# A kernel of two transformer blocks with 32 experts: a fixed order for the loop over pairs of experts, another beginning of the experts' stage, and weights in chunks of half a matrix

## The chip, the cores and the metric

One core of a Trainium2 chip. The metric is the time of one execution on the device in microseconds; the kernel before ran three times: 1050.86, 1051.72 and 1053.38 us, median 1051.72.

## The reference

Two transformer blocks over 256 tokens of width 1024, all in f32. The first has two kinds of attention and a gated FFN with a convolution. The second has two kinds of attention and then a mixture of experts, and only that is touched:

```python
h2 = modulate(rmsnorm(x, g_ffn), shift_ffn, scale_ffn)
group = argmax(softmax(h2 @ w_group))                 # 4 groups
p, e = top_k(softmax((h2 @ w_expert)[group]), 2)      # 2 of the 8 experts of the group
y = sum over the 2 of: weight * ((silu(h2 @ w_gate[e]) * (h2 @ w_up[e])) @ w_down[e])
out = rmsnorm(x + gate_ffn * y, g_final)
```

There are 32 experts; w_gate and w_up of one are 1024 x 512, w_down is 512 x 1024, 2 MB each: 192 MB (of 1,048,576 bytes) in all, each read once.

## The kernel before, in words

All large weights come through one ring of 1 MB buffers (8 KB a partition). `plan` (L405) lists the chunks in the order of their use, `pump` (L150) issues the next chunk's load on SyncE's queue as soon as a buffer is free, and `done` gives a chunk's buffer back when its last product is issued. SyncE's queue is in program order; the order on the other engines is chosen by the tile framework's scheduler when the kernel is built, except that instructions given to `pin` keep their program order among each other. The ring has 10 buffers and gets others as earlier stages give them up: 17 ahead of the experts' stage, an 18th when the transposed x (`xT`, buffer WHL[0]) has been read, a 19th when x has been added to the accumulators.

The experts go in 16 pairs. A chunk of a pair is a quarter of one matrix of both experts: `w_pair` (L344 issues) takes for each partition one run of 4 KB of each expert, that is two rows k of gate or up, or one row of down. A pair has 12 chunks: four of gate, four of up, four of down.

`moe` (L1480 on) begins with the residual (L1497), the squares of x and their root (`squares`, `root`: L235, L240, L241), and the transposes of x on TensorE (L206) whose copies to SBUF (L1508, L1510) give xT. `route` (L1303 on) has per block of 128 tokens: logits by 16 products with xT, then a chain of VectorE steps (L1310 to L1327), a short product that counts tokens per expert, and their ranks `rk` (L1336). A generator is stepped by the string `'a2 q1 a4 ...'`. Pair 0 gets its 2 x 64 token places by products with a selection matrix (`selects` L1523, `row`), in f32, as soon as the ranks are there. For the other pairs `normed` (L1534, L1535) makes x times its root as a high and a low fp32r part, `places` (L1545) makes the 0/1 matrix `hot`, and `gather` multiplies the two and lets ScalarE modulate the result into `xt` (L1539). Pairs are gathered in groups (0), (1,2), (3,4), ..., (13,14), (15).

The loop over pairs then has for pair pr, as written: gate products (`times_x`, 32 TensorE instructions), half 0 of `combine` of pair pr-1 (products that add the weighted output into the four accumulator banks), `weighted` of that pair's half 1 (L1475 to L1477), up products, half 1 of `combine`, silu and product (`gated`, L1593, L1594), `slots` (transposes of `hot` and the slots' weights, L1573, L1576), `places` of the next group, `act_T` (four transposes and two copies, L1604), `gather` of the next group in every second pair, `down` (32 instructions). Two pairs of PSUM banks, 4 to 7, take turns. For pair 15 a branch comes first (`rest_of_experts`, for experts with more than 64 tokens; it isn't entered here), and then the load of the last gain. The final norm follows (L1703 to L1708). TensorE's instructions are all recorded at the helpers' lines, L203 for products and L206 for transposes.

Of the kernel before, what the change touches and what calls it, by code (L numbers as in the profile page):

```python
# [111 lines left out]
class Kernel:  # L112
# [12 lines left out]


# [75 lines left out]
    def mm(self, out, lhsT, rhs, start, stop):  # L202
        return self.nc.tensor.matmul(out, lhsT, rhs, start=start, stop=stop, skip_group_check=True)  # L203

    def tr(self, out, in_, ident):
        return self.nc.tensor.transpose(out, in_, ident)  # L206
# [139 lines left out]

    def w_tiles(self, src, r0):
# [57 lines left out]
    def plan(self):  # L405
# [1063 lines left out]
    def weighted(self, ps, w, gate, hf, y):  # L1469
# [5 lines left out]
        nc.vector.scalar_tensor_tensor(tmp[:n], ps, w, gate[:n, cs], op0=ALU.mult, op1=ALU.mult)  # L1475
        nc.scalar.activation(y[:, 0], tmp[:n], AF.Copy)  # L1476
        nc.vector.tensor_tensor(y[:, 1], tmp[:n], y[:, 0], op=ALU.subtract)  # L1477

    def moe(self):
# [37 lines left out]
        def selects(pr, tb, pin=lambda i: i):  # L1517

            s = self.t([128, 128], "sel", tag="diag", bufs=2)
            sel[tb] = s  # L1520
            for e in range(2):
                n = 2 * pr + e
                pin(nc.vector.scalar_tensor_tensor(s[:, e * 64:e * 64 + 64], self.iota1, self.rk[:, tb, n:n + 1],  # L1523
                                                   r2[:, tb:tb + 1].to_broadcast([128, 64]), op0=ALU.is_equal,
                                                   op1=ALU.mult))
# [53 lines left out]
        def times_x(pr, n, b):  # L1579
            ps = self.bank(b)  # L1580
            for k in range(KT):
# [5 lines left out]
                if k % 2:  # L1587
                    self.done(c)
# [180 lines left out]
```

## Time and profile before

| | |
|---|---|
| median of 3 runs | 1051.72 us |
| the profiled execution's own time | 1051.73 us |
| its span, first to last instruction | 1049.9 us |
| TensorE busy, share of the span | 983.1 us, 94% |
| VectorE, ScalarE, GpSimd busy | 515.7, 407.3, 47.1 us |
| mean granted TensorE clock | 0.983 |
| bytes moved by DMA | 313.51 MB, mean 299 GB/s |

The busy times are sums over stages with different limits. The experts' stage begins at 558 us. What limits it is read from its own stretches: how full the DMA stream is, what TensorE waits for, and what comes last. A share of DMA above 1 means that packets of one engine overlap a little. Times in the rows are us from the start of the span.

### The profile page before, as it was taken

The page shows a single profiled execution, that of the slowest core. Times are in us where ns is not written, and L with a number is a line of the kernel's source. Part 1 is how long each engine was busy: PE and PEld are TensorE (multiplying, and loading weights), DVE is VectorE, ACT ScalarE, POOL GpSimd, SP SyncE. Part 2 cuts the span into 40 slices and gives each one's busy share as a digit, 9 for nine tenths or more (in the row PEclk, how much of TensorE's full clock was granted, in tenths as well). Part 3 has the DMA queues.
Part 4 walks back from the last instruction along what each step waited for, and adds up shares of the span by engine and source line. Part 5 has one row for each costly group of instructions (what it writes and reads, how often), then busy time and mean ns, then how long its engine had stood idle before and what let it go on. Part 6 is the DMA issues. An engine that isn't in the chain of part 4 may idle for free. (4 is left out here: it accounts for less than half of the span.)

```text
span 1049.9 us, 14498 instructions
## 1 busy us (share of the span) xinstructions
PE 983.1 (94%) x5815; PEld 672.5 (64%) x5815; DVE 515.7 (49%) x940; ACT 407.3 (39%) x751; POOL 47.1 (4%) x48
## 2 busy tenths in 40 slices
PE   5999899999999998899987999999899999999996
PEld 5997599999999996789766535334343334333342
DVE  5658688979889876656796111111111110111112
ACT  5566566555555555455653311111020202011022
POOL 2000200000000001000061000000000000000000
PEclk9999999999999999899998999999999999999999
DMA  7964655967777867554644799999999999999995
GB/s 202 368 236 128 226 202 165 315 230 256 267 250 235 287 230 269 204 164 151 254 148 134 275 409 409 409 408 409 409 409 409 410 409 409 409 409 409 409 407 207
DMA packets 131519, 313.51 MB, mean 299 GB/s; under 512 B 7229, under 2 KB 59226, under 8 KB 131450
## 3 DMA queue, kind: packets, MB, share of 16 engines
q1 hardware_dynamic: 131082, 312.02, 80.0%
q0 software_dynamic: 368, 0.54, 0.3%
q8 instruction: 46, 0.75, 0.3%
q14 instruction: 23, 0.19, 0.0%
HBM read 311.89 MB, written 1.05 MB: 298 GB/s over the span
## 5 line engine op out<-in xcount | busy, mean ns | idle before, releaser
L203 PE MATMUL bank<-buf,buf 128*128 128x256 f32 (+4 forms) x4152 | 703.4, 381 | 8.0 <-DVE buf L277 2.6
L203 PEld LDWEIGHTS bank<-buf,buf 128*128 128x128 f32 (+1 forms) x4152 | 493.8, 176 | 176.4 <-issue 124.0
L178 DVE TENSOR_TENSOR buf<-buf,buf 128x1024 fp32r<-128x1024 f32 x150 | 183.2, 1222 | 57.7 <-ACT buf L176 54.7
L176 ACT ACTIVATE buf<-buf 128x1024 fp32r<-128x1024 f32 x154 | 162.2, 1054 | 93.6 <-PE bank L203 82.1
L203 PE MATMUL bank<-buf,aT 128*64 128x512 f32 x512 | 114.8, 595 | 3.3 <-ACT aT L1604 3.3
L1594 DVE TENSOR_TENSOR act<-act,bank 128x512 f32<-128x512 f32 x16 | 11.0, 688 | 208.4 <-PE bank L203 208.4
L1475 DVE SCALAR_TENSOR_TENSOR tmp<-bank,wslot,gffn 128x512 f32<-128x512 f32 x32 | 24.0, 751 | 133.0 <-PE bank L203 131.2
L203 PEld LDWEIGHTS bank<-buf,aT 128*64 128x64 f32 x512 | 37.0, 137 | 69.4 <-issue 59.6
L1593 ACT ACTIVATE act<-bank 128x512 f32<-128x512 f32 x16 | 9.6, 597 | 135.4 <-PE bank L203 135.4
L1476 ACT ACTIVATE buf<-tmp 128x512 fp32r<-128x512 f32 x32 | 20.2, 631 | 107.5 <-DVE tmp L1475 107.5
L949 ACT ACTIVATE buf<-bank,convT 128x256 f32<-128x256 f32 x64 | 36.0, 563 | 54.3 <-PE bank L203 42.5
L1539 ACT ACTIVATE buf<-bank,mod,g_ffn 128x256 f32<-128x256 f32 (+1 forms) x72 | 34.6, 538 | 48.6 <-PE bank L203 48.6
L1604 ACT ACTIVATE aT<-bank 128x256 f32<-128x256 f32 x32 | 10.5, 382 | 95.1 <-PE bank L206 95.1
L203 PE MATMUL bank<-buf,ST 128*128 128x512 f32 x128 | 38.2, 420 | 8.0 <-ACT buf L1476 7.9
L203 PEld LDWEIGHTS bank<-buf,ST 128*128 128x128 f32 x128 | 21.5, 188 | 36.8 <-ACT buf L1476 18.5
L203 PEld LDWEIGHTS bank<-hot,buf 128*128 128x128 f32 x256 | 32.0, 189 | 17.1 <-issue 8.9
L1045 DVE SCALAR_TENSOR_TENSOR bank<-buf,c,bank 128x512 f32<-128x512 f32 x56 | 41.9, 749 | 0.6 <-DMA buf<-in_w_ada_dram 0.3
L203 PE MATMUL bank<-hot,buf 128*128 128x256 f32 (+1 forms) x256 | 36.6, 290 | 3.6 <-ACT act L1593 3.6
L206 PE MATMUL bank<-base,buf 128*128 128x128 f32 x128 | 21.1, 312 | 18.0 <-DVE buf L260 7.8
L951 DVE SCALAR_TENSOR_TENSOR buf<-bank,convT,buf 128x255 f32<-128x255 f32 x64 | 30.6, 478 | 7.8 <-ACT buf L949 7.4
L206 PEld LDWEIGHTS bank<-base,buf 128*128 128x128 f32 x128 | 17.8, 176 | 21.1 <-DVE buf L260 7.8
L953 DVE SCALAR_TENSOR_TENSOR buf<-bank,convT,buf 128x254 f32<-128x254 f32 x64 | 30.6, 478 | 1.1
(203 smaller groups left out, 629.3 us busy)
## 6 DMA issues: line engine op xcount, KB each, us to landing
buf<-in_w_up_dram SPq DMA_DIRECT2D x96, 1024.0 KB, 18.1
buf<-in_w_down_dram SPq DMA_DIRECT2D x79, 1024.0 KB, 18.2
buf<-in_w_gate_dram SPq DMA_DIRECT2D x64, 1024.0 KB, 18.3
buf<-in_w_ada_dram SPq DMA_DIRECT2D x24, 1024.0 KB, 7.3
buf<-in_w_in_dram SPq DMA_DIRECT2D x18, 1024.0 KB, 9.8
buf<-in_w_out_dram SPq DMA_DIRECT2D x8, 1024.0 KB, 16.7
buf<-in_w_in_dram SPq DMA_DIRECT2D x6, 512.0 KB, 7.7
buf<-in_x_dram SPq DMA_DIRECT2D x2, 512.0 KB
```

Of the source, the lines that this page charges most:

```text
L176: pin(nc.scalar.activation(H, raw, AF.Copy))
L178: pin(engine.tensor_tensor(L, raw, H, op=ALU.subtract))
L203: return self.nc.tensor.matmul(out, lhsT, rhs, start=start, stop=stop, skip_group_check=True)
L206: return self.nc.tensor.transpose(out, in_, ident)
L949: nc.scalar.activation(c[:, s, :], u[:, s, :], AF.Identity, scale=cT[:, 128 + n:129 + n], bias=cT[:, 192 + n:193 + n])
L951: nc.vector.scalar_tensor_tensor(c[:, s, 1:], u[:, s, 0:255], cT[:, 64 + n:65 + n], c[:, s, 1:], op0=ALU.mult, op1=ALU.add)
L953: nc.vector.scalar_tensor_tensor(c[:, s, 2:], u[:, s, 0:254], cT[:, n:n + 1], c[:, s, 2:], op0=ALU.mult, op1=ALU.add)
L1045: nc.vector.scalar_tensor_tensor(p.pa, w, s, p.pa, op0=ALU.mult, op1=ALU.add)
L1475: nc.vector.scalar_tensor_tensor(tmp[:n], ps, w, gate[:n, cs], op0=ALU.mult, op1=ALU.mult)
L1476: nc.scalar.activation(y[:, 0], tmp[:n], AF.Copy)
L1539: nc.scalar.activation(xt[:, k, :n], g, AF.Identity, scale=A[:, k:k + 1], bias=B[:, k:k + 1])
L1594: nc.vector.tensor_tensor(act, act, u, op=ALU.mult)
```

## The change

Three parts. (1) The loop over pairs issues gate, silu, up, product, both halves of combine of the pair before, transposes of act, slots, gather, down and both halves of weighted, in this order, and while `self.ordered` is set every instruction of it on TensorE, VectorE and ScalarE keeps its program order. All pairs are gathered in groups of two, (0,1) to (14,15). (2) The beginning: both blocks' squares, copies and roots first; `normed` and pair 0's own f32 products are gone; instead xT is transposed back on TensorE (`back`) and its high and low parts are made from PSUM (`high`, `low`), and the first group's `gather` does all high parts first. Routing steps of the two blocks are interleaved by a new string. All four residual products come in pair 0 of the loop. (3) A chunk of gate, up and down is now half of one matrix of one expert: for each partition one run of 8 KB (`w_half`). Only the four down chunks of pair 15 keep the old form. The bytes and their order by matrix are the same.

```diff
+    def kept(self, i):
+        return self.pin(i) if self.ordered else i
...
+    def w_half(self, src, k, half):
+
+        n = src.shape[1] * k // 2
+        v = src.rearrange("(p k) c -> p (k c)", k=k)[:, half * n:half * n + n]
+
+        def load(t):
+            self.nc.sync.dma_start(t, v)
         return load
...
-                    load = self.w_pair(w[2 * pr:2 * pr + 2], k, part, 2 if (pr, n, part) == (15, "down", 3) else 1)
-                    self.experts[n, pr, part] = self.add_raw(n, load)
+                    if (pr, n) == (15, "down"):
+                        c = self.add_raw(n, self.w_pair(w[2 * pr:2 * pr + 2], k, part, 2 if part == 3 else 1))
+                        c.left = 2
+                        for e in range(2):
+                            self.experts[n, 2 * pr + e, part] = c, e * D
+                    else:
+                        e, half = part % 2, part // 2
+                        c = self.add_raw(n, self.w_half(w[2 * pr + e], k, half))
+                        c.left = k // 2
+                        for i in range(k // 2):
+                            self.experts[n, 2 * pr + e, k // 2 * half + i] = c, i * 2048 // (k // 2)
...
-        self.row_rstd(halves[0], r2[:, 0:1], self.pin)
+        pin = self.pin
         for tb in range(TB):
+            ss = self.squares(halves[tb], pin)
...
-                if tb and not half:
-                    nc.vector.tensor_copy(to, pt)
+                if half:
+                    pin(nc.vector.tensor_copy(to, pt))
                 else:
-                    self.pin(nc.scalar.activation(to, pt, AF.Copy))
-        ss = self.squares(halves[1], self.pin)
-        acc = [[self.bank(0), self.bank(1)], [self.bank(2), self.bank(3)]]
-        ST, W, sel = {}, {}, {}
-        groups = [(0,)] + [(i, i + 1) for i in range(1, 15, 2)] + [(15,)]
+                    pin(nc.scalar.activation(to, pt, AF.Copy))
+            self.root(ss, r2[:, tb:tb + 1], pin)
+        ST, W = {}, {}
+        groups = [(i, i + 1) for i in range(0, 16, 2)]
...
+        def back(tb):
+
+            pts = []
+            for half in range(2):
+                pt = self.bank((2, 3, 0, 1)[2 * tb + half], (128, 4, 128))
+                for kk in range(4):
+                    pin(self.tr(pt[:, kk, :], xT[:, half * 4 + kk, tb * 128:tb * 128 + 128], self.ident))
+                pts.append(pt)
+            return pts
+
+        def high(tb, half):
+
+            pin(nc.scalar.activation(xn[0][:, tb, half * 4:half * 4 + 4], turned[tb][half], AF.Copy,
+                                     scale=r2[:, tb:tb + 1]))
+
+        def low(tb, half):
+            ks = slice(half * 4, half * 4 + 4)
+            pin(nc.vector.scalar_tensor_tensor(xn[1][:, tb, ks], turned[tb][half], r2[:, tb:tb + 1], xn[0][:, tb, ks],
+                                               op0=ALU.mult, op1=ALU.subtract))
...
+        def gather(group, banks, first=False):
+
+            s = hot[:, where[group[0]][0]]
+            g = [self.bank(b, (128, 2, 256)) for b in banks]
+
+            def part(i, n):
+                for j in range(2):
+                    for tb in range(TB):
+                        self.mm(g[i][:, j, :], xn[n][:, tb, 2 * i + j, :], s[:, tb], n + j + tb == 0, n + tb == 2)
+            if first:
+                for i in range(4):
+                    part(i, 0)
+            for i in range(4):
+                if not first:
+                    part(i, 0)
+                part(i, 1)
+                for j in range(2):
+                    modulate(2 * i + j, g[i][:, j, :], 256)
...
         def times_x(pr, n, b):
             ps = self.bank(b)
             for k in range(KT):
-                c = self.experts[n, pr, k // 2]
                 for e in range(2):
-                    c0 = e * D + (k % 2) * 512
-                    self.mm(ps[e * 64:e * 64 + 64, :], xt[:, k, where[pr][1] + e * 64:where[pr][1] + e * 64 + 64], c.tile[:, c0:c0 + 512],
-                            k == 0, k == KT - 1)
-                if k % 2:
+                    c, c0 = self.experts[n, 2 * pr + e, k]
+                    self.mm(ps[e * 64:e * 64 + 64, :], xt[:, k, where[pr][1] + e * 64:where[pr][1] + e * 64 + 64], c.tile[:, c0:c0 + 512], k == 0, k == KT - 1)
                     self.done(c)
             return ps
...
         def down(pr, aT, banks):
             ps = [self.bank(b) for b in banks]
             for i in range(4):
-                c = self.experts["down", pr, i]
                 for hf in range(2):
                     for e in range(2):
-                        c0 = e * D + hf * 512
+                        c, c0 = self.experts["down", 2 * pr + e, i]
+                        c0 += hf * 512
                         self.mm(ps[hf][e * 64:e * 64 + 64, :], aT[i // 2][:, i % 2, e * 64:e * 64 + 64],
                                 c.tile[:, c0:c0 + 512], i == 0, i == 3)
-                self.done(c)
-            self.weighted(ps[0], W[pr], gate, 0, y[0])
-            return ps[1]
+                for e in range(2):
+                    self.done(self.experts["down", 2 * pr + e, i][0])
+            for hf in range(2):
+                self.weighted(ps[hf], W[pr], gate, hf, y[hf])
...
-        for what in 'a2 q1 a4 b1 r0 a1 b1 r1 a1 b1 s0 b1 h0 b2 b1 h1 b1 s1'.split():
+        turned = {}
+        for what in 'a4 b1 a2 t0 b1 h00 a1 t1 b1 a1 p0 h01 b3 b1 b1 p1 h10 h11 l00 l10 l01 l11'.split():
...
+            elif what[0] == "t":
+                turned[n] = back(n)
+            elif what[0] == "p":
+                self.ordered = True
+                places(groups[0], n)
+                self.ordered = False
...
+                {"h": high, "l": low}[what[0]](n, int(what[2]))
+        gather(groups[0], (6, 7, 4, 5), True)
         self.give(WHL[0])
         for tb in range(TB):
             self.expert_weights(tb, self.logits[tb])
-        normed()
-        places(groups[0])
-        second = None
+        acc = [[self.bank(0), self.bank(1)], [self.bank(2), self.bank(3)]]
+        self.ordered = True
         for pr in range(16):
-            banks, others = ((4, 5), (6, 7))[::1 if pr % 2 == 0 else -1]
-            if pr < 15:
-                g = times_x(pr, "gate", banks[0])
-            if pr:
-                combine(pr - 1, 0, False)
-                self.weighted(second, W[pr - 1], gate, 1, y[1])
-            if pr < 15:
-                u = times_x(pr, "up", banks[1])
-            if pr:
-                combine(pr - 1, 1, False)
-            else:
-                for hf in range(2):
-                    residual(1, hf)
-                self.give(X)
-                self.blocks_left()
+            banks, others = ((6, 7), (4, 5))[::1 if pr % 2 == 0 else -1]
+            group = next((gr for gr in groups if gr[0] == pr + 1), None)
             if pr == 15:
                 assert self.next_dma == len(self.chunks)
+                for hf in range(2):
+                    combine(pr - 1, hf, False)
+                self.ordered = False
                 self.rest_of_experts(xn, A, B, gate, acc, self.free[:3])
                 gfin = self.buf(self.free[3], [128, D])
                 fin = self.buf(self.free[4], [128, TB, D])
                 nc.sync.dma_start(gfin, bass.AP(tensor=a["g_final_2"].tensor, offset=a["g_final_2"].offset,
                                                 ap=[[0, 128], [1, D]]))
-                g, u = times_x(pr, "gate", banks[0]), times_x(pr, "up", banks[1])
-            act = gated(g, u)
+                self.ordered = True
+            if group:
+                for tb in range(TB):
+                    places(group, tb)
+            g = times_x(pr, "gate", banks[0])
+            act = silu(g)
+            u = times_x(pr, "up", banks[1])
+            gated(act, u)
+            if not pr:
+                for tb in range(TB):
+                    for hf in range(2):
+                        residual(tb, hf)
+                self.ordered = False
+                self.give(X)
+                self.blocks_left()
+                self.ordered = True
+            elif pr < 15:
+                for hf in range(2):
+                    combine(pr - 1, hf, False)
+            aT = act_T(pr, act, others[0])
             slots(pr, others[1])
-            group = next((gr for gr in groups if gr[0] == pr + 1), None)
-            if group:
-                places(group)
-            aT = act_T(pr, act, others[0])
             if group:
                 gather(group, banks + others)
-            second = down(pr, aT, banks)
-        self.weighted(second, W[15], gate, 1, y[1])
+            down(pr, aT, banks)
         for hf in range(2):
             combine(15, hf, True)
```

## Rows read from the trace of the kernel before

**Rows 1.** busy by stage: stretch, length, engines, clock, DMA share, GB/s

```profile
604.00:1030.00 426.00, 401.76 (x1923) 168.59 (x1920) 64.48 (x128) 65.08 (x130) 0.00 (x0) 1.00 1.03 409
```

**Rows 2.** waits of TensorE, its weight loads, 700-1000: total, times, longest

```profile
PE bank L206 <- DVE act L1594: 8.6, 10, 0.9
...
PEld bank L203 <- DMA buf<-in_w_down_dram: 1.9, 6, 0.4
```

**Rows 3.** timeline of TensorE, pairs 2 to 4: start, us, what, count

```profile
635.19 7.18 PE L203 MATMUL bank<-buf,buf 128*64 128x512 f32 x31
...
663.37 7.04 PE L203 MATMUL bank<-buf,buf 128*64 128x512 f32 x32
...
688.20 3.60 PE L203 MATMUL bank<-buf,buf 128*64 128x512 f32 x16
```

**Rows 4.** timeline of TensorE, starts of pairs 10 and 12

```profile
864.61 1.94 PE L203 MATMUL bank<-buf,buf 128*64 128x512 f32 x8
...
923.22 1.94 PE L203 MATMUL bank<-buf,buf 128*64 128x512 f32 x8
```

**Rows 5.** SyncE's issues: first after the pause, last; its landing

```profile
583.93 2.08 SPq L344 DMA_DIRECT2D buf<-in_w_up_dram  x2
...
1017.64 6.04 SPq L344 DMA_DIRECT2D buf<-in_w_down_dram  x1
...
buf<-in_w_down_dram SPq DMA_DIRECT2D x1, 512.0 KB, 19.2
```

**Rows 6.** the chain that ended last: pair 15's gate and up, its down

```profile
1015.99 13.97 PE bank L203 x64
...
1032.02 7.11 PE bank L203 x32
```

**Rows 7.** timeline of the experts' beginning, all engines

```profile
558.28 2.73 DVE L1497 SCALAR_TENSOR_TENSOR buf<-bank,rstd,buf 128x512 f32<-128x512 f32 x4 [0.82 <-POOL rstd L220]
...
561.75 2.16 ACT L1534 ACTIVATE buf<-buf,r 128x1024 fp32r<-128x1024 f32 x1
...
562.06 3.66 PE L203 MATMUL bank<-wr,buf 128*128 128x40 f32 x32
...
563.94 2.08 DVE L1535 SCALAR_TENSOR_TENSOR buf<-buf,r,buf 128x1024 fp32r<-128x1024 f32 x1 [1.44 <-ACT buf L1534]
...
565.95 0.24 DVE L1310 SCALAR_TENSOR_TENSOR logits<-bank,r,rc 128x40 f32<-128x40 f32 x1
566.22 0.49 DVE L1315 TENSOR_TENSOR rdif<-logits 128x320 f32<-128x320 f32 x1
...
576.29 0.19 DVE L1336 SCALAR_TENSOR_TENSOR rk<-bank,pick 128x32 f32<-128x32 f32 x1 [1.95 <-PE bank L203]
...
581.95 13.95 PE L203 MATMUL bank<-buf,buf 128*64 128x512 f32 x64
```

**Rows 8.** busy by stage around the routing, columns as in 1

```profile
565.00:570.00 5.00, 3.00 (x13) 1.35 (x12) 3.36 (x10) 2.86 (x3) 0.80 (x1) 1.00 0.60 193
570.00:575.00 5.00, 1.71 (x7) 1.71 (x8) 4.34 (x11) 0.00 (x0) 0.00 (x0) 0.55 0.04 16
...
580.00:585.00 5.00, 5.00 (x23) 2.88 (x24) 0.83 (x6) 4.42 (x10) 0.00 (x0) 0.93 0.05 5
```

**Rows 9.** timeline, gather of pairs 1, 2: products and modulations

```profile
599.10 3.99 PE L203 MATMUL bank<-hot,buf 128*128 128x256 f32 x32
...
600.39 3.82 ACT L1539 ACTIVATE buf<-bank,mod,g_ffn 128x256 f32<-128x256 f32 x8 [0.35 <-PE bank L203]
```

**Rows 10.** DMA packets of 8-15, 30-37, 57.5-64, 700-1000 us

```profile
DMA packets 4075, 2.05 MB, mean 293 GB/s; under 512 B 63, under 2 KB 4075, under 8 KB 4075
...
DMA packets 2417, 2.44 MB, mean 348 GB/s; under 512 B 36, under 2 KB 2417, under 8 KB 2417
...
DMA packets 1252, 2.50 MB, mean 385 GB/s; under 512 B 37, under 2 KB 37, under 8 KB 1251
...
DMA packets 31798, 122.73 MB, mean 409 GB/s; under 512 B 1869, under 2 KB 1869, under 8 KB 31786
```

More of the change, by code (lines that the diff above doesn't have):

```diff
@@ L1517, in selects @@
[L1517 to L1525, printed above, removed]
-        def row(pr, g, tb, k, start):
-            return self.mm(g[k // 4][:, k % 4, :], x[tb][:, k, :], sel[tb], start, tb == 1)
@@ L1531, in normed @@
-        def normed():
-            for tb in range(TB):
-                nc.scalar.activation(xn[0][:, tb], x[tb], AF.Copy, scale=r2[:, tb:tb + 1])
-                nc.vector.scalar_tensor_tensor(xn[1][:, tb], x[tb], r2[:, tb:tb + 1], xn[0][:, tb], op0=ALU.mult,
-                                               op1=ALU.subtract)
+                if half:
+                    pin(nc.vector.tensor_copy(to, pt))
+                else:
+                    pin(nc.scalar.activation(to, pt, AF.Copy))
+            self.root(ss, r2[:, tb:tb + 1], pin)
@@ L1547, in places @@
                                         self.rk[:, tb, 2 * group[0]:2 * group[0] + n, None].to_broadcast([128, n, 64]),
-                                        op=ALU.is_equal)
-        def gather(group, banks):
-            n = 128 * len(group)
-            each = 512 // n
-            s = hot[:, where[group[0]][0], :, :n]
-            for i in range(KT // each):
-                g = self.bank(banks[i], (128, each, n))
-                for j in range(each):
-                    for part in range(2):
-                        for tb in range(TB):
-                            self.mm(g[:, j, :], xn[part][:, tb, i * each + j, :], s[:, tb], part + tb == 0,
-                                    part + tb == 2)
-                for j in range(each):
-                    modulate(i * each + j, g[:, j, :], n)
+                                        op=ALU.is_equal))
@@ L1603, in act_T @@
             for i in range(2):
[L1604 removed]
+                self.kept(nc.scalar.activation(aT[i], pt[:, 2 * i:2 * i + 2, :], AF.Copy))
             return aT
@@ L1625, in residual @@
         def residual(tb, hf):
-            self.pin(self.mm(acc[tb][hf], self.ident, self.x[:, tb, hf * 512:hf * 512 + 512], True, False))
+            self.mm(acc[tb][hf], self.ident, self.x[:, tb, hf * 512:hf * 512 + 512], True, False)
         self.logits = []
         route = [self.route(tb, xT, r2[:, tb:tb + 1]) for tb in range(TB)]
-        g = [self.bank(6 + half, (128, 4, 128)) for half in range(2)]
-        def steps(tb, n):
-            for _ in range(n):
-                next(route[tb])
-        def first_rows(tb, ks):
-            for k in ks:
-                self.pin(row(0, g, tb, k, tb == 0 and k % 4 == 0))
-        for what in 'a2 q1 a4 b1 r0 a1 b1 r1 a1 b1 s0 b1 h0 b2 b1 h1 b1 s1'.split():
+        turned = {}
+        for what in 'a4 b1 a2 t0 b1 h00 a1 t1 b1 a1 p0 h01 b3 b1 b1 p1 h10 h11 l00 l10 l01 l11'.split():
             n = int(what[1])
             if what[0] in "ab":
-                steps("ab".index(what[0]), n)
-            elif what[0] == "q":
-                self.root(ss, r2[:, 1:2])
-            elif what[0] == "r":
-                residual(0, n)
-            elif what[0] == "s":
-                selects(0, n, self.pin)
-            else:
-                first_rows(0, range(4 * n, 4 * n + 4))
-        first_rows(1, range(KT))
-        for k in range(KT):
-            modulate(k, g[k // 4][:, k % 4, :], 128)
+                for _ in range(n):
+                    next(route["ab".index(what[0])])
+            elif what[0] == "t":
[4 more added lines that the diff above has]
+                self.ordered = False
+            else:
+                {"h": high, "l": low}[what[0]](n, int(what[2]))
+        gather(groups[0], (6, 7, 4, 5), True)
         self.give(WHL[0])
```

31 lines of the change are left out of this document (16 added, 15 removed).

## The prediction

> **What bounds the kernel now.** I read the busy table by stage first. In the stretch from 604 to 1030 us the DMA engines move 409 GB/s at a share of 1.03, while TensorE is busy for 401.76 of 426 us and VectorE for 64.48 [rows 1]. So nearly half of the span runs at the pace of the experts' weights. I then asked who makes TensorE wait there. Between 700 and 1000 us its longest sum is 8.6 us behind VectorE's act (ten waits of up to 0.9 us); the waits of its weight loads for w_down come to 1.9 us in six waits of up to 0.4 us [rows 2]. The reader should see both: the stream never rests, yet TensorE hardly ever waits for a chunk. That is so because the chunks run ahead, and the timeline of TensorE shows why they still do at 900 us. Early on, pair 2 starts at 635.19, pair 3 at 663.37 and pair 4 at 688.20: 28.2 us with a gather behind the pair and 24.8 us without, 53.0 us for two [rows 3]. Later the order is another: products of the gather and of combine stand between those of gate, and two pairs take 923.22 - 864.61 = 58.6 us [rows 4]. A pair's 12 chunks need 12 x 1.0486 MB / 409 GB/s = 30.8 us. So TensorE at 29.3 us a pair gains only 1.5 us a pair on the stream and has caught up just about when the kernel ends. There the two meet: the last chunk's second piece is issued at 1017.64 and lands 19.2 us later, at 1036.8 [rows 5]; the last down product ends at 1032.02 + 7.11 = 1039.1 [rows 6]. The end is thus the end of the stream plus 2.3 us of TensorE plus the final norm. **Two things can move it: when the stream starts again, and how fast it flows.** A faster TensorE alone can win at most those 2.3 us.
>
> **When it starts.** In the chunk queue 18 chunks are loaded before the experts' stage; the next is issued at 583.93 [rows 5], 2.0 us after the first gate product (581.95 [rows 7]), when the first slot is free. Before that, DMA moves 16 GB/s between 570 and 575 us [rows 8].
>
> **The new beginning.** From the residual at 558.28 to gate 0 the old one takes 23.7 us [rows 7]. Two things stand in its way. The normed halves go first: 2.16 us on ScalarE at 561.75 ahead of a copy that xT needs, and 2.08 us on VectorE at 563.94 ahead of routing, which so starts at 565.95; a second pair of them follows, and the second block's ranks come at 576.29 [rows 7]. Then pair 0 has f32 products of its own. In the new order both blocks' squares, copies and roots are pinned first. The 32 routing products take 3.66 us from 562.06 [rows 7]; I let them start at 562.2, when both copies of block 0 are out, so block 0's logits are there at 564.1 and block 1's at 565.9. VectorE then has for each block three steps of 0.49 us and four of 0.19 to 0.24, some 2.3 us [rows 7], and one place, a step over 256 elements to the 320 of a routing step, at 0.4: 5.4 us for both; I add 1.1 us for two short rank products that it waits for, so 564.1 + 6.5 = 570.6. The sixteen transposes back and the four high parts lie on TensorE and ScalarE inside that time. The first gather is 32 products; such a gather takes 3.99 us, and its eight modulations 3.82 us on ScalarE, one step behind [rows 9]. The four low parts (0.68 us each, as the four residual steps at 558.28 that take 2.73 [rows 7]) run during its first 16 products. Gate 0 starts at about 574.7.
>
> **The first release.** A chunk now holds four k of one expert, and two chunks are read side by side, so nothing is free before half of gate is done: 64 products take 13.95 us [rows 7], a quarter of them 3.5 us. First issue: 578.2 instead of 583.93, a gain of **5.7 us**. After that two slots come free each 3.5 us, 1.75 us a chunk, which is faster than the stream takes them. Here lies one unknown, TensorE's clock. [...] If it falls as before, the gather takes 8 us and gate runs at half speed until the clock is back, some 0.7 us into the stretch from 580 with its mean of 0.93 [rows 8]: first issue at about 583, a gain of 0.8 us.
>
> **The rate.** The size of one row of a load is the size of its packets. Four stretches with a full stream show what a packet costs, as 16 engines x size / rate [rows 10]: 512 B at 293 GB/s gives 28 ns, 1 KB at 348 gives 47 ns, 2 KB at 385 gives 85 ns, 4 KB at 409 gives 160 ns. The steps are 19, 38 and 75 ns: 37 ps a byte, and about 10 ns a packet whatever its size. So a packet of 8 KB would take 160 + 2 x 75 = 310 ns, and a chunk 8 x 310 = 2.484 us instead of 16 x 160.2 = 2.564. Of the 174 chunks behind the restart the four of the last down keep 4 KB: 170 x 0.080 = **13.6 us less**. No load in this trace has rows of 8 KB, so this is an extrapolation, one doubling beyond the last row; its ends are 0 (no gain) and 170 x 8 x 10.8 ns = 14.7 us (the constant as the 2 KB and 4 KB rows alone give it). I take 13.6, since four sizes lie on one line.
> [...]
>
> **The fixed order in the loop.** On TensorE a pair is now gate, up, combine, four transposes, slots, gather in every second pair, down, as in the early rows, so I cost it as those: 53.0 us for two pairs [rows 3]. Combine covers VectorE's product, slots cover the copies of the transposed act, down covers the modulations. That is 26.5 us a pair against 12 x 2.484 = 29.8 us of the stream. So TensorE catches up by mid-stage and then waits for chunks; that costs nothing, as the stream sets the end. Two more residual products in pair 0 (about 1 us) and the pair 15 that shares a gather with pair 14 (2 us less) drown in this slack; VectorE and ScalarE have more of it. Slots: 19 in all, of which TensorE holds four or so, enough to keep the stream full. The load into xT's buffer waits for the transposes back, some 3 us later than now, with nothing needed behind it on SyncE's queue before 578.
>
> **The tail.** The last gate and up chunks come in pairs too. After up's last one lands, half of up is left (3.5 us), then act, transposes and copies (about 2.6 us), then 7.1 us of down: 13.2 us, while four down chunks take 10.3. So TensorE ends 2.9 us behind the last landing, not 2.3: **+0.6 us**.
>
> **Sum.** The profiled execution's own time is 1051.73, the median of three 1051.72, so they stand as one. 1051.73 - 5.7 - 13.6 + 0.6 = **1033.0 us**. With the clock down: 1037.9.
>
> **Rivals.** *The rate stays at 409*: the stream has a ceiling of its own at the source, or the queue cuts rows at 4 KB. For it: no larger row was seen. Against: the straight line. Then 1051.7 - 5.7 + 0.6 = 1046.6, or 1051.5 with the clock down. *The fixed order is the bound*: every pair waits for VectorE and ScalarE in line. TensorE starts at 574.7, pair 0 takes some 27 us, and combine and the branch ahead of pair 15 about 5; pair 15's gate starts at 1015.99 now [rows 6], so the time stays as it is if 574.7 + 27 + 14 P + 5 = 1016, which is P = 29.2 us a pair. At 30.2 us (each pair exposing act's 0.9, copies' 0.5, combine's 0.7 and about 1.6 us of modulations) the kernel ends 14 us later, at 1066: slower. For it: the old order reaches 29.3. Against: rows of the early pairs have the same order at 26.5, and TensorE would have to lose 2.7 us a pair. *Between*: such waits cost part of it, P around 28.5 to 29, 1042 to 1050.
>
> **How the numbers follow.** Forecast with the clock held 0.46; the same with the clock down 0.26; rate stays 0.13; between 0.07; order slower than now 0.05; the rest is for what I don't see. 0.2% of this time is 2.1 us, about what a measurement can tell: faster takes the first two, two thirds or more of the third, and most of the fourth, 0.89; same 0.05; slower 0.06. The range from 1029 (1 us more from the rate, 3 us from a beginning or tail better than worked out) to 1047 holds the first two, most of the third and of the fourth; what is left out is about 0.15.
>
> **What would show it.** Right: 421 to 424 GB/s in the middle of the stage, waits of TensorE's weight loads for chunks of many us in the later pairs, first release near 578, last landing near 1018, two pairs of 53 to 54 us before TensorE has caught up. Wrong: 409 GB/s again, or TensorE without waits for chunks to the end at 29 us or more a pair, or a granted clock of 0.5 that reaches into gate 0.

## The result, and the profile after

The changed kernel takes 1035.57 us in the median of four runs (1033.66 to 1041.14), the kernel before 1051.83 beside it: a ratio of 0.9856, 95% interval 0.9837 to 0.9875. Repeated twice, four runs each, it came to 0.987 (0.9851 to 0.989) and 0.9884 (0.9868 to 0.99), medians 1038.83 and 1040.01. It is faster by 1.2 to 1.4%, and the 1033.0 us of the prediction lie 2.6 us below the first median and 5.8 and 7.0 below the others. The profiled execution is the longest of the first four, 1041.14 us with a span of 1039.4; all rows of after come from it.

**The stream.** Busy by stage, the stretch that answers to [rows 1], and the DMA packets of 700 to 1000 us, which answer to the last of [rows 10]:

```profile
604.00:1000.00 396.00, 375.44 (x1825) 166.28 (x1821) 63.42 (x128) 62.96 (x127) 0.00 (x0) 1.00 1.01 420
```

```profile
DMA packets 17283, 125.95 MB, mean 420 GB/s; under 512 B 1919, under 2 KB 1919, under 8 KB 1919
```

420 GB/s instead of 409: nearly all weight packets are now 8 KB, half as many as before. The share of busy DMA time is 1.01, where it was 1.03.

**Who waits.** Waits of TensorE, and below them of its weight loads, between 700 and 1000 us (total, times, longest), to be held against [rows 2]:

```profile
PE bank L205 <- DMA buf<-in_w_up_dram: 11.3, 9, 1.3
PE bank L205 <- DMA buf<-in_w_gate_dram: 6.0, 6, 2.3
...
PEld bank L205 <- DMA buf<-in_w_up_dram: 23.3, 20, 2.2
PEld bank L205 <- DMA buf<-in_w_gate_dram: 11.8, 9, 3.2
```

The picture has turned round: no line for VectorE's act is left, and what TensorE waits for is chunks. The reason is in its timeline, pairs 2 to 4, as [rows 3]:

```profile
629.82 13.90 PE L205 MATMUL bank<-buf,buf 128*64 128x512 f32 x64
653.66 13.90 PE L205 MATMUL bank<-buf,buf 128*64 128x512 f32 x64
681.40 4.03 PE L205 MATMUL bank<-buf,buf 128*64 128x512 f32 x18
```

23.8 us without a gather, 27.7 with one, 51.6 for two pairs where 53.0 and later 58.6 stood. TensorE has caught up with the stream by pair 7, whose 64 products of gate and up take 14.55 us from 756.82 on where pair 6 has 13.90, and from there on follows it.

**The beginning**, all engines, as [rows 7]:

```profile
560.50 2.73 DVE L1520 SCALAR_TENSOR_TENSOR buf<-bank,rstd,buf 128x512 f32<-128x512 f32 x4 [0.82 <-POOL rstd L225]
...
566.27 0.26 DVE L1333 SCALAR_TENSOR_TENSOR logits<-bank,r,rc 128x40 f32<-128x40 f32 x1 [1.03 <-PE bank L205]
...
571.44 0.19 DVE L1359 SCALAR_TENSOR_TENSOR rk<-bank,pick 128x32 f32<-128x32 f32 x1 [0.50 <-PE bank L205]
...
572.25 3.56 PE L205 MATMUL bank<-hot,buf 128*128 128x256 f32 x28 [0.17 <-DVE hot L1566]
...
575.74 1.51 PE L205 MATMUL bank<-buf,buf 128*64 128x512 f32 x6
```

From the residual to gate 0 it is 575.74 - 560.50 = 15.2 us where 23.7 stood; the second block's ranks come 10.9 us after the residual instead of 18.0. In this execution the stages ahead ended late: the residual is at 560.50, 2.2 us after that of before, while in the next profile of the same kernel it is at 557.98. The granted clock stays at 1.00, where [rows 8] had 0.55 (columns as in [rows 1]):

```profile
565.00:570.00 5.00, 5.00 (x47) 4.93 (x46) 3.76 (x13) 1.81 (x4) 0.56 (x1) 1.00 0.00 0
570.00:575.00 5.00, 4.27 (x31) 3.71 (x31) 4.36 (x12) 1.51 (x4) 0.00 (x0) 1.00 0.62 210
```

SyncE's issue that waits for the first free slot, as the first of [rows 5], stands at 579.41, 18.9 us after the residual (before 25.65):

```profile
579.41 0.80 SPq L358 DMA_DIRECT2D buf<-in_w_up_dram  x2
```

**The end.** Timeline of TensorE, pair 15's gate and up and its down, against [rows 6] (in brackets the idle time ahead and what ended it; "issue" means nothing that the trace can name):

```profile
997.19 1.47 PE L205 MATMUL bank<-buf,buf 128*64 128x512 f32 x5 [0.41 <-PEq L1397]
1002.63 14.79 PE L205 MATMUL bank<-buf,buf 128*64 128x512 f32 x59 [3.97 <-issue]
...
1019.51 7.09 PE L205 MATMUL bank<-buf,aT 128*64 128x512 f32 x32
```

The last chunk's second piece lands at 1019.20, but TensorE is 7.4 us behind it (1019.51 + 7.09 = 1026.60; before 2.3 behind). Five products into pair 15's gate it stops for 3.97 us, and the granted clock then falls (columns as in [rows 1]):

```profile
1000.00:1005.00 5.00, 2.37 (x8) 0.84 (x10) 0.00 (x0) 0.00 (x0) 0.00 (x0) 0.82 1.01 412
1005.00:1010.00 5.00, 5.00 (x22) 1.47 (x20) 0.00 (x0) 0.00 (x0) 0.00 (x0) 0.84 1.01 407
```

The spans add up so, set against the forecast with the clock held:

| | predicted | before to after | difference |
|---|---|---|---|
| first issue for a free slot | -5.7 | 583.93 to 579.41 | -4.5 (6.7 nearer to the residual) |
| from there to the last landing | -13.6 | 452.94 to 439.79 | -13.2 |
| TensorE's end behind that | +0.6 | 2.26 to 7.40 | +5.1 |
| down's end to the span's end | 0 | 10.8 to 12.8 | +2.0 |
| sum | -18.7 | 1049.9 to 1039.4 | -10.5 |

So the two gains came and the tail took back 7 us. Taken from the residual to the end of the span, so that the stages ahead drop out, it is 1049.9 - 558.3 = 491.6 us before and 1039.4 - 560.5 = 478.9 after. Two questions were left for runs: does the fixed order really cost and bring nothing, and what is the pause?

### The profile page after: what moved, and what is told of

Read it like the earlier page. It is cut to its first block, busy times and chain, and to the rows that moved or that the text cites. A ratio compares the mean times of both kernels' runs of the same rounds, so it can differ in the third digit from the quotient of the medians.

```text
span 1039.4 us, 14468 instructions
## 1 busy us (share of the span) xinstructions
PE 978.5 (94%) x5799; PEld 675.3 (65%) x5799; DVE 514.1 (49%) x937; ACT 400.6 (39%) x744; POOL 46.8 (4%) x48
## 5 line engine op out<-in xcount | busy, mean ns | idle before, releaser
L205 PE MATMUL bank<-buf,buf 128*128 128x256 f32 (+4 forms) x4152 | 710.9, 383 | 27.5 <-DMA buf<-in_w_up_dram 11.3
L205 PEld LDWEIGHTS bank<-buf,buf 128*128 128x128 f32 (+1 forms) x4152 | 502.4, 178 | 223.7 <-issue 139.3
L1629 ACT ACTIVATE aT<-bank 128x256 f32<-128x256 f32 x32 | 10.5, 381 | 158.1 <-PE bank L208 158.1
L1499 ACT ACTIVATE buf<-tmp 128x512 fp32r<-128x512 f32 x32 | 20.1, 629 | 125.8 <-DVE tmp L1498 125.8
L208 PE MATMUL bank<-base,buf 128*128 128x128 f32 x144 | 24.4, 319 | 16.8 <-DVE buf L265 7.7
L1561 ACT ACTIVATE buf<-bank,mod,g_ffn 128x256 f32<-128x256 f32 x64 | 30.9, 561 | 10.2 <-PE bank L205 10.2
L208 PEld LDWEIGHTS bank<-base,buf 128*128 128x128 f32 x144 | 20.5, 175 | 20.1 <-DVE buf L265 7.7
L205 PE MATMUL bank<-hot,buf 128*128 128x256 f32 x256 | 32.8, 284 | 0.6 <-DVE rk L1359 0.3
L1500 DVE TENSOR_TENSOR buf<-tmp,buf 128x512 fp32r<-128x512 f32 x32 | 22.1, 692 | 22.4 <-ACT buf L1499 22.4
## 6 DMA issues: line engine op xcount, KB each, us to landing
buf<-in_w_up_dram SPq DMA_DIRECT2D x96, 1024.0 KB, 19.9
buf<-in_w_down_dram SPq DMA_DIRECT2D x79, 1024.0 KB, 19.9
buf<-in_w_gate_dram SPq DMA_DIRECT2D x64, 1024.0 KB, 19.9
buf<-in_w_out_dram SPq DMA_DIRECT2D x8, 1024.0 KB, 17.2
```

Of the source, the lines that this page charges most:

```text
L205: return self.kept(self.nc.tensor.matmul(out, lhsT, rhs, start=start, stop=stop, skip_group_check=True))
L208: return self.kept(self.nc.tensor.transpose(out, in_, ident))
L1499: self.kept(nc.scalar.activation(y[:, 0], tmp[:n], AF.Copy))
L1500: self.kept(nc.vector.tensor_tensor(y[:, 1], tmp[:n], y[:, 0], op=ALU.subtract))
L1561: self.kept(nc.scalar.activation(xt[:, k, :n], g, AF.Identity, scale=A[:, k:k + 1], bias=B[:, k:k + 1]))
```

## The experiments

The changed kernel ran again, and one part at a time was undone; a run of before with the chunks alone stands beside them. Then come runs on the pause.

**The changed kernel, unchanged.** 

> The changed kernel once more, nothing edited. Expected: 1034 to 1037 us. Its profiled execution was the slowest of its four (1041.14), and in it TensorE stood still for 3.97 us behind the branch of pair 15 with no releaser, and the granted clock fell for 3.4 us right after. Theory: that pause belongs to single executions; if so the next profile is without it and its span is about 5 us shorter. Rival: every execution has it, and the spread comes from the stages before the experts.

1038.83 us (1036.09 to 1039.65), ratio 0.987. Its trace has the same marks: residual 557.98, first issue 576.88, last landing 1017.01, a pause of 4.27 us, down's end 7.3 us behind the last landing. So the pause doesn't belong to a single execution, and the forecast for this run was too low. From the residual to the end of the span it is 479.1 us here, 478.9 in the first trace and 478.5 in a third further down: the three differ by 0.6 us, while the residual itself stands at 557.98, 560.50 and 558.55. In the traced executions the spread comes from the stages ahead of the experts, as the rival said. The differences below are against this run.

**Chunks of the same form in two runs of 4 KB.**

```diff
-        n = src.shape[1] * k // 2
-        v = src.rearrange("(p k) c -> p (k c)", k=k)[:, half * n:half * n + n]
+        v = src.rearrange("(p a b k) c -> p b a (k c)", a=2, b=2, k=k // 4)[:, half]
...
-            for k in range(KT):
+            for k in (0, 1, 4, 5, 2, 3, 6, 7):
```

> Only the packet size is undone: a chunk is still half of one matrix of one expert, but its rows are every other quarter, so that each partition reads two runs of 4 KB with a gap between them (the products take k in that order). Theory (a packet costs about 10 ns whatever its size): the stream falls back to 409 GB/s, 2.564 us a chunk, and the end comes 170 x 0.08 = 13.6 us later: 1047 to 1050 us. Rival (what counts is that a chunk comes from one matrix, not the packet): 420 GB/s and 1034 to 1037 us.

1046.77 us (1045.95 to 1050.4), ratio 0.9949 (0.9933 to 0.9966). The packets of 700 to 1000 us:

```profile
DMA packets 31789, 122.69 MB, mean 409 GB/s; under 512 B 1870, under 2 KB 1870, under 8 KB 31776
```

409 GB/s again, with all else kept but the order in which the products take k: it is the row size that sets the rate here, 409 with 4 KB and 420 with 8 KB. The last landing moves from 1017.01 to 1029.15, 12.1 us; the medians differ by 7.9, which puts this run just below its forecast (its profiled execution is over 3 us longer than any other of its four, and why isn't shown).

**Fixed order undone.**

```diff
-        self.ordered = True
         for pr in range(16):
...
-                self.ordered = True
...
-                self.ordered = True
```

> Only the fixed order of the loop is undone: the instructions stand in the program as in the changed kernel, but the scheduler may move them. Theory (at 29.3 us a pair, as in the late pairs of before, TensorE would hold up a stream that needs 29.9): TensorE hardly waits for chunks and the end is its own, 6 to 10 us later, 1042 to 1046 us. Rival (the fixed order is worth nothing, since the stream sets the end with any order): 1034 to 1037 us, with waits for chunks as now.

1058.24 us (1055.39 to 1059.71), ratio 1.0051 (1.0029 to 1.0072): slower than before, though its stream runs at 420 GB/s and its last chunk lands at 1018.67, as in the changed kernel. The order that the scheduler makes is the bound. Timeline of TensorE, two pairs apart (a pair begins with two products of gate), and its longest waits between 700 and 1000 us:

```profile
868.93 1.07 PE L205 MATMUL bank<-buf,buf 128*64 128x512 f32 x2
...
930.97 1.07 PE L205 MATMUL bank<-buf,buf 128*64 128x512 f32 x2
```

```profile
PE bank L208 <- DVE act L1620: 8.5, 10, 0.9
PE bank L205 <- ACT buf L1499: 6.5, 10, 0.7
PE bank L205 <- DVE wslot L1602: 4.2, 5, 0.8
```

62.0 us for two pairs, 31.0 a pair, where the scheduler's order of before had 29.3 [rows 4] and I had expected it again. No line names a chunk; TensorE falls behind the stream by its own order. Its waits for other engines are not the whole of it: in these 300 us they come to 25.0 us, 2.6 a pair, against 21.1 or 2.1 a pair before, 8.6 of them in [rows 2]. The rest of the 1.7 us by which a pair is longer than before is time that the trace counts as busy (28.5 us a pair against 27.2). What makes the products take longer there isn't shown.

**The kernel before with the new chunks alone** (`w_half`, its plan, and the loops that read it).

> The kernel before with the new chunks alone: old beginning, old loop, free order. Theory: the stream would be done 12 us sooner (13.6 less, 1.75 later at its start), but TensorE in the old order needs 29.3 us a pair and starts when it did, so the gain is only what it waits for chunks now plus the 2 us by which the stream is late at the end: 1048 to 1052 us, with TensorE not waiting for chunks in the late pairs. Rival (the stream alone sets the end): 1039 to 1041 us.

1069.79 us (1068.82 to 1069.97), ratio 1.0171 (1.0154 to 1.0188). I was wrong by some 20 us, for the same reason:

```profile
873.32 1.07 PE L203 MATMUL bank<-buf,buf 128*64 128x512 f32 x2
...
935.38 1.07 PE L203 MATMUL bank<-buf,buf 128*64 128x512 f32 x2
```

Again 62.1 us for two pairs, at 420 GB/s and with the last landing at 1024.25. The new chunks alone make the kernel slower: with them the scheduler's order takes 31.0 us a pair where it took 29.3. What in its rules does that was not tried.

**Old beginning.** Squares, `normed`, pair 0's products, `residual`, route string and copies of the kernel before, in the changed kernel; pair 0 has its own 128-token products again, and the groups are the old ones, (0), (1,2) to (13,14), (15).

> Only the new beginning is undone: the old one (normed halves in ScalarE's and VectorE's way, f32 products of pair 0, old groups) with the fixed order of the loop and chunks of 8 KB rows. Theory (the end is the restart of the stream plus 174 chunks): from the residual to gate 0 it takes 23.7 us again, not 15.2 to 17.4, and the first slot comes free 25.4 us behind the residual, not 18.9; the end comes 6 to 8.5 us later: 1043 to 1047 us. Rival (the beginning is hidden behind chunks already loaded): 1036 to 1039 us.

1045.11 us (1043.09 to 1046.33), ratio 0.9939 (0.9919 to 0.9959). Residual, then busy by stage (columns as in [rows 1]), then gate 0:

```profile
555.62 2.73 DVE L1520 SCALAR_TENSOR_TENSOR buf<-bank,rstd,buf 128x512 f32<-128x512 f32 x4 [0.82 <-POOL rstd L225]
...
570.00:575.00 5.00, 4.38 (x19) 4.38 (x19) 2.78 (x15) 0.23 (x1) 0.00 (x0) 0.50 0.00 0
...
579.27 13.95 PE L205 MATMUL bank<-buf,buf 128*64 128x512 f32 x64
```

23.65 us from the residual to gate 0, at the lower clock, as in [rows 7] and [rows 8]. In time the beginning is worth 1045.11 - 1038.83 = 6.3 us, or 7.3 by the ratios (0.9939 - 0.987). To the stream it is worth more. The first free slot is issued at 582.95, 27.3 us after the residual and not the 25.4 expected, since with the new chunks half of gate has to be done first; that is 8.4 us behind the 18.9 of the new beginning, and the last landing (1023.87) is 9.2 us later, taken from the residual. But this kernel has no pause in pair 15, and its down ends 4.7 us behind the last landing and not 7.3, which hides a part.

**The branch ahead of pair 15 left out.** The code for experts with more than 64 tokens is left out; with these inputs it isn't entered.

```diff
-                self.rest_of_experts(xn, A, B, gate, acc, self.free[:3])
```

> The branch for experts with more than 64 tokens is left out of the changed kernel (with these inputs it isn't entered), so no engine branches ahead of pair 15. Theory (the pause of 3 to 4 us behind the branch is TensorE waiting for its code, and pair 15 starts late by it; the granted clock falls because of it): no pause, no fall of the clock, and the end comes 4 to 6 us sooner: 1030 to 1034 us. Rival (the code would be late with or without the branch, or the stream sets the end there anyway): 1036 to 1039 us.

1034.4 us (1031.99 to 1035.86), ratio 0.9842 (0.9822 to 0.9862). Gate and up of pair 15 run without a gap:

```profile
993.52 14.80 PE L205 MATMUL bank<-buf,buf 128*64 128x512 f32 x64
```

Down ends 2.6 us behind the last landing. The pause belongs to the branch; it costs 4.4 us by the medians, 2.9 by the ratios (0.987 - 0.9842). The intervals of the two ratios overlap, so the traces are the better witness: from the residual to the end of the span it is 473.3 us here against 479.1. The granted clock did fall, to 0.5 from 991.85 to 995.26, which was not expected without a pause.

**The branch kept, its body cut to two instructions.** Left out: the same experts.

> The changed kernel with the branch kept and its body cut to two instructions; left out: the experts with more than 64 tokens, whose code is not entered with these inputs. Theory: TensorE's pause of 3 to 4.3 us in pair 15 is the fetch of the code that lies behind the long body; with a short body the code is there, the pause is under 1 us, TensorE's clock does not fall because of it, and the time is 1033 to 1036, as without the branch. Rival: the branch itself (reading the count, the engines meeting there) costs the pause; then 3 to 4 us of pause stay in front of gate's products and the time is 1037 to 1040, as the changed kernel.

1033.9 us (1033.08 to 1035.56), ratio 0.9834 (0.9817 to 0.9851). Timeline of TensorE behind the branch:

```profile
994.92 7.08 PE L205 MATMUL bank<-buf,buf 128*64 128x512 f32 x30
1002.30 8.16 PE L205 MATMUL bank<-buf,buf 128*64 128x512 f32 x32 [0.30 <-PEq L1397]
...
1012.55 7.09 PE L205 MATMUL bank<-buf,aT 128*64 128x512 f32 x32
```

No pause, clock at 1.00, down's end 2.5 us behind the last landing. This run changes one thing more than was meant: TensorE now takes gate's products ahead of the branch and only up's behind it. But the branch is there, with 0.30 us of waiting, and in the changed kernel the wait at the branch itself is 0.41 us and the pause comes five products later. So reading the count and meeting at the branch isn't what costs. What is left is the code behind a long body. The DMA part of the trace has rows for it (packets, MB, share of 16 engines); these are of the changed kernel between 998.66 and 1002.63 us, its pause:

```profile
q8 instruction: 1, 0.02, 1.7%
q14 instruction: 1, 0.01, 0.5%
```

One packet of instructions of 16 KB and one of 8 KB come in the pause, among the weights' packets. The large one ends at 1001.35, and TensorE goes on 1.28 us later. In the four other traces with a pause (the changed kernel twice more, the 4 KB chunks, and the quarters below) that distance is 1.25 to 1.47 us. In these five traces no packet of 16 KB comes between 33 us ahead of pair 15's gate and 2.1 us behind its start. Five traces of kernels that have the long body and no pause each have one shortly ahead of the gate: the kernel before at 1009.54, 6.4 us ahead of the gate at 1015.99, the old beginning at 997.80, 7.6 us ahead of 1005.41, and the three runs below with combine moved 3.6 to 4.6 us ahead. Each of them has another 2.9 to 4.1 us behind gate's start, and TensorE goes on without a pause. So what differs between these five traces and those five is whether the earlier packet came, and moving code moves it. That TensorE waits for its code is an inference from these times; no row names that wait.

The body is jumped over here, and TensorE does four to nine products behind the branch before it stops. The price is 3.0 to 4.3 us in four traces and 1.8 in a fifth, beside a full stream (404 GB/s at a DMA share of 1.00 in the changed kernel's pause). The prediction has no rival with a pause behind the branch: the trace of before shows none, only the 0.75 us of waiting at the branch itself.

**Combine of pair 14 behind up of pair 15.** The branch then follows pair 14's down at once, and the pause can lie beside VectorE's steps.

```diff
-                for hf in range(2):
-                    combine(pr - 1, hf, False)
                 self.ordered = False
                 self.rest_of_experts(xn, A, B, gate, acc, self.free[:3])
...
-            elif pr < 15:
+            else:
```

> In pair 15 combine of pair 14 comes behind up, as in all other pairs, and not ahead of the branch. Theory: gate 15 then starts about 5 us sooner, since it waits neither for the weighted output of pair 14 (some 2 us) nor for combine (2.9 us), and combine covers the product in front of the transposes; the pause behind the branch stays but falls into slack; TensorE ends 3 us behind the last landing, not 7.4: 1031 to 1034 us. Rival (the pause moves the clock and the rest eats the gain): 1036 to 1039 us.

1035.32 us (1034.7 to 1037.89), ratio 0.9854 (0.9833 to 0.9874). One wait of 4.25 us is left, behind VectorE at the branch, and no second one:

```profile
994.23 16.42 PE L205 MATMUL bank<-buf,buf 128*64 128x512 f32 x64 [4.25 <-DVEq L1397]
```

Down's end is 3.5 us behind the last landing. The 16 KB packet comes inside the wait (990.61 to 991.71). Gate 15 does not start 5 us sooner, as was expected, but 0.6 (436.1 us after the residual, 436.6 in the trace of the changed kernel beside it); what is won is that TensorE doesn't stop again behind it: from gate's start to down it is 19.4 us, with combine in them, and 22.6 in that other trace without.

**Pair 0's gate in quarters.** The first slot is free after a quarter of gate's products, not after half.

```diff
+                    if (pr, n) in ((0, "gate"),):
+                        c = self.add_raw(n, self.w_pair(w[2 * pr:2 * pr + 2], k, part))
+                        c.left = 2 * (k // 4)
```

> The four chunks of pair 0's gate keep the old form, a quarter of both experts' matrices, all else as in the changed kernel; they are loaded long before the stage. Theory: the first slot comes free after an eighth and not a quarter of the 64 products, 1.75 us sooner, and the whole stream and the end with it: 1.5 to 2 us less, 1034 to 1037 us if the changed kernel stands at 1037. Rival (the end hangs on TensorE in pair 15, not on the stream): no change.

1037.35 us (1033.0 to 1038.97), ratio 0.9866 (0.9842 to 0.9889): not told apart from the changed kernel. In the trace the stream ends at 1013.87, and down begins only there, with a pause of 4.18 us ahead of it. Most of that early end is the residual's, which stands at 555.91. Taken from the residual, the first slot is issued after 17.2 us instead of 18.9, but the last landing comes after 458.0 where the three traces of the changed kernel have 458.7 to 459.0: the stream keeps 0.7 to 1.1 of the 1.7 us, and down ends 7.1 us behind it as in the changed kernel.

**Both parts.** 

> The changed kernel with both parts tried apart: combine of pair 14 behind up of pair 15 (so the branch follows pair 14's down at once), and pair 0's gate in the old quarter chunks, so that the first slot is free 1.75 us sooner. If the end is the later of the stream and TensorE's last pairs, the stream should end near 1014 from the start of the span, as with the quarters alone, and the tail behind it be shorter than the 7.1 us of that run, because the wait at the branch runs beside VectorE's steps: down of pair 15 ends some 4 to 5 us behind the last landing, time 1032 to 1035. If the pause behind the branch stays in full, it is 1036 to 1038, no better than the quarters alone.

1033.91 us (1032.53 to 1035.74), ratio 0.9832 (0.9814 to 0.985); last landing 1016.16, not near 1014 (458.4 us after the residual), down's end 3.5 us behind it.

Then both kernels once more, side by side. **The changed kernel:** 

> The changed kernel again, on the same chip and in the same rounds as the kernel with both parts, because its two medians so far (1035.6 and 1038.8 us) lie further apart than the difference to be settled. Expected 1035 to 1039, TensorE's pause behind the branch 3 to 4.3 us, down of pair 15 ending 7 to 8 us behind the last landing.

1040.01 us (1038.8 to 1040.96), ratio 0.9884 (0.9868 to 0.99), above the forecast. Gate of pair 15 in its trace, from 990 to 1010 us:

```profile
995.81 2.79 PE L205 MATMUL bank<-buf,buf 128*64 128x512 f32 x5 [0.41 <-PEq L1397]
1000.36 10.01 PE L205 MATMUL bank<-buf,buf 128*64 128x512 f32 x38 [1.76 <-issue]
```

The pause is only 1.76 us, and down still ends 7.1 us behind the last landing (1017.21). The granted clock fell ahead of the pause here (it is 0.5 from 993.45 to 1003.69), so the first five products took 2.79 us instead of 1.47; TensorE goes on 1.33 us after the 16 KB packet, as in the other traces.

**Both parts:** 

> The kernel with both parts (combine of pair 14 behind up of pair 15, pair 0's gate in quarters) again, beside the changed kernel. If both parts are worth what the traces show (1 us or so of the stream, 3 to 4 us of the tail), it is 3 to 5 us below the changed kernel of the same call: 1032 to 1035. If the medians differ by under 2 us, the gain is not settled by these runs.

1035.53 us (1034.02 to 1036.16), ratio 0.9838 (0.9824 to 0.9851). Its TensorE at the end:

```profile
992.41 12.88 PE L205 MATMUL bank<-buf,buf 128*64 128x512 f32 x50 [4.25 <-DVEq L1403]
...
1012.36 7.09 PE L205 MATMUL bank<-buf,aT 128*64 128x512 f32 x32
```

4.5 us below the changed kernel on the same chip, and the intervals don't meet: this version beats both kernels, with all of the computation in it. By the traces the gain is the place of combine. The quarters bring nothing that shows: the last landing is 458.9 us after the residual here and 458.7 in the changed kernel beside it.

## Why the prediction was right, and where it was off

**The rate: right.** 8 KB packets were worked out at 422 GB/s from the line through four smaller sizes, and 420 came; 13.6 us were forecast from restart to last landing, and 13.2 are in the trace. The 4 KB run, back at 409 GB/s, shows that it is the row size. The upper end of this term, 14.7 us, took a constant of 10.8 ns a packet; the 2 KB and 4 KB rows that it names give 10.0, and so 13.6 again.

**The beginning: right.** The clock held, at 1.00 from 565 to 580 us. The sum's 5.7 us takes it to hold, which no run ahead of the forecast shows: [rows 8] has 0.55 there. The second block's places were due 12.3 us after the residual and were done after 11.6, gate 0 was due after 16.4 us and came after 15.2, the first issue after 19.9 and came after 18.9. Undone alone, the part is worth 6.3 us of time and 8.4 us of the stream's restart. The forecast of 5.7 had the later first release of the new chunks in it (3.5 us behind gate 0 instead of 2.0); without that it is 7.2.

**The fixed order: right in its pace, wrong in its worth.** The sentence "that costs nothing, as the stream sets the end" held: 51.6 us for two pairs, forecast 53.0. But costing it at nothing took for granted that without it the old order of 29.3 us a pair would stand. It doesn't: with the new chunks the scheduler makes 31.0, and the same change without the fixed order is slower than before. The order is worth 1058.24 - 1038.83 = 19.4 us, the largest part of the change, and all of it is spent on holding the other two parts' gain. The rival "the fixed order is the bound" is refuted; the free order is.

**The tail: the term that was mis-sized.** "+0.6 us" was +7.1 in the profiled execution, and +7.0 in the next profile. Of that, 5.1 are TensorE's distance to the last landing. The step's own working (13.2 us from the last up landing to the end of down against 10.3 of stream) is right where there is no pause: 2.5 us behind with the short body, 2.6 without the branch, forecast 2.9. What failed is that the branch ahead of pair 15 was priced as part of "about 5" in a rival and at nothing in the sum, because in the trace of before it costs 0.75 us in front of the gate. That trace couldn't show the pause; I didn't ask whether moved code changes what the branch costs. With the tail at +7.1 the sum gives 1039.5, where the two later medians lie (1038.83 and 1040.01); that the first median is only 2.6 us off the forecast is, by the traces, luck. The other 2.0 us lie behind down. The fixed order puts VectorE's last subtraction for half 0 ahead of the first step of half 1. Timeline of VectorE, before and then after, and ScalarE after:

```profile
1038.30 1.61 DVE L1475 SCALAR_TENSOR_TENSOR tmp<-bank,wslot,gffn 128x512 f32<-128x512 f32 x2 [6.95 <-PE bank L203]
1039.82 1.48 DVE L1477 TENSOR_TENSOR buf<-tmp,buf 128x512 fp32r<-128x512 f32 x2
```

```profile
1025.78 0.75 DVE L1498 SCALAR_TENSOR_TENSOR tmp<-bank,wslot,gffn 128x512 f32<-128x512 f32 x1 [5.51 <-PE bank L205]
1027.23 0.69 DVE L1500 TENSOR_TENSOR buf<-tmp,buf 128x512 fp32r<-128x512 f32 x1 [0.69 <-ACT buf L1499]
1027.84 0.74 DVE L1498 SCALAR_TENSOR_TENSOR tmp<-bank,wslot,gffn 128x512 f32<-128x512 f32 x1
...
1029.91 0.68 DVE L1500 TENSOR_TENSOR buf<-tmp,buf 128x512 fp32r<-128x512 f32 x1
```

```profile
1028.58 0.60 ACT L240 ACTIVATE junk<-bank 128x512 bf16<-128x512 f32 x1 [1.38 <-PE bank L205]
...
1029.16 0.62 ACT L1499 ACTIVATE buf<-tmp 128x512 fp32r<-128x512 f32 x1
```

Half 1 is ready 4.0 us after down's end instead of 2.2. Its first step starts 1.2 us after down's end, where before both halves' steps came one behind the other; the other 0.6 us go to a step of the final norm (L240) that ScalarE takes ahead of half 1's copy (L1499). The prediction costed "both halves of weighted" only inside the loop, where down of the next pair covers it; behind pair 15 nothing covers it. Turning the two steps round was not tried.

What stays open: why the changed kernel's own runs spread over 1033.66 to 1041.14. The three traced ones all have the pause and differ by their residuals; for the others, the spans alone don't tell whether they have it, or when their residual came.

## What to carry to other kernels

This stream of 1 MB loads gained from longer rows up to the 8 KB that were tried (409 GB/s with 4 KB, 420 with 8 KB), and the gain could be worked out from the sizes that the trace already had; but whoever speeds up the stream has to ask at once whether the compute order keeps up, and a scheduler's order must be measured again after each change, not carried over. A branch late in a kernel is worth trying beside work that other engines still have to finish: here down then ended 3.5 us behind the last landing instead of 7.1 to 7.4. Steps that a loop covers have to be priced once more for its last turn.

## What the runs showed of the hardware that was not expected

TensorE stood still a few products behind a branch that isn't entered, for 3.0 to 4.3 us in four traces and 1.8 in a fifth, and went on 1.25 to 1.47 us after a 16 KB packet of instructions had come through the DMA engines beside the weights (DMA share 1.00 in the changed kernel's pause). The granted clock fell to 0.5 in each of the five: just behind the pause in two, within it in two, and ahead of it in the one with 1.8 us. From the first product of pair 15's gate to the first of its down it is 22.3 us in the changed kernel, and 16.05 in the one with the old beginning, which has the same order there and no pause. The clock can fall there without a pause too (0.5 from 991.85 to 995.26 in the run without the branch, behind the short waits for combine), so it is not the pause's alone.
